# A two-layer encoder: sums of weight quarters for the down projection made ahead, in DRAM

## The chip, the cores and the metric

The kernel runs on one core of a Trainium2 chip. The metric is device time in microseconds of one execution; times shown are medians over runs. The engines are named as in the profile: PE (TensorE matmul), PEld (its weight loads), DVE (VectorE), ACT (ScalarE), POOL (GpSimd), SP (SyncE, which here only issues DMAs).

## The reference

A batch of one sequence of 512 tokens with 1024 features passes two layers. The mixer of layer 0 is neighbourhood attention over an 8 x 64 grid of tokens, that of layer 1 a mixture of three dilated sliding-window attentions. Everything is float32. Cut to what matters here:

```python
D_MODEL, SEQ, DEPTH = 1024, 512, 2
D_FF = 2816

def swiglu(x, w_gate, w_up, w_down):
    return (jax.nn.silu(x @ w_gate) * (x @ w_up)) @ w_down

# every layer:
#   x += post_norm(mixer(pre_norm(x)))
#   x += post_norm(swiglu(pre_norm(x)))
```

The change concerns `@ w_down`, a product of a 512 x 2816 matrix with a 2816 x 1024 one, once in each layer.

## The kernel before, in words

The program is one long sequence: queries, keys and values with the attention of layer 0; its output projection; gate and up of layer 0; down of layer 0; the same for layer 1 with the dilated attention. A scheduler orders the instructions of each engine by priorities and dependences when the program is built, so neighbouring stages overlap on an engine.

Every large product is done with seven half-size products in place of eight (the method of Strassen and Winograd), and every factor is split into a high and a low part (`split`: an ACT copy, L89, and a DVE subtraction, L90), which `mm3` multiplies in three matmuls, L101 to L103. The products of four quarters need sums of quarters of both factors.

For attention projections and gate and up this is done per unit by the class `Seven`: a unit loads two weight halves of 512 KB (`load2`, L85, on SP's queue), and its method `sums` adds quarters of the weights, two of the additions on POOL (L168, L169, and for some units L170 and L174). Gate and up has 22 units f in each layer, the neighbourhood attention 8 units j of queries and keys, the dilated attention 24 units n.

For the down projection, `down`, the weight `wd` lies in DRAM as four quarters `ga`, `gb`, `ua`, `ub` of 128 x 5632 floats (2·QF, with QF = 2816). The seven products are, in this order: p2 with gb; p1 with ga; d1 with ga+ua; s2 with ga+ua+ub, and between its pieces s4 with ub; s3 with ua+ub; x2b with all four. The chain's names of tiles carry them: `h_d0p`, `l_d0p` are the high and low parts for p1 and p2 of layer 0, `h_d0d` those for d1, `h_d0s` for s2, s3 and s4, `h_d0x2b` for x2b; layer 1 has `h_d1...`. Each product goes in 6 pieces, five of 128 x 1024 floats (512 KB, 12 matmuls of 128 x 512) and one of half that. The results gather in the PSUM tiles `yd_s` (left) and `yd_pp` (right).

Before, the sums are made within the down projection. The arena `mem` (named `wd`) holds ga, which SP loads with L652; accumulating DMAs of POOL's queue (L604, in `add`) put ua onto it for d1, ub for s2, gb for x2b. For s3 a piece of ua is loaded into a ring buffer and ub accumulated onto it. That is 24 accumulating DMAs a layer. Plain loads (L610, in `loaded`) go through a ring of four half buffers `r_d`, the same memory that gate and up's units use, and from d1 on two more in the arena `more` (named `raw`).

The arenas `wd` and `raw` reuse the memory of `fg`, which gate and up used; the last instruction that reads `fg` is L568, the product that makes the last tile of `hid`, the input of down.

Of the kernel before, what the change touches and what calls it, by code (L numbers as in the profile page):

```python
# [12 lines left out]
F32 = mybir.dt.float32  # L13
# [25 lines left out]
def encoder_kernel(ctx: ExitStack, tc: tile.TileContext, a: dict, out: bass.AP):  # L39
# [88 lines left out]
    class Seven:  # L128
# [36 lines left out]
        def sums(self):  # L165
            q, e = self.q, self.adds
            self.w22 = split(*self.v, q[3])
            e[0].tensor_add(q[0], q[0], q[2])  # L168
            e[1].tensor_add(q[2], q[2], q[3])  # L169
            e[2].tensor_add(q[3], q[0], q[3])  # L170
            self.w12 = self.pair("b", self.q3[:, 0:4:3])
# [367 lines left out]
        pre(3)  # L539
        ops(3)  # L540

    def gate_up(layer, xs, hid, fg):
        wg, wu = a["wg"], a["wu"]
        raws = ring(fg, 0, 2 * D, 3)
        g_, u_, p5_ = ring(fg, 6 * D, 512, 4), ring(fg, 8 * D, 512, 2), ring(fg, 9 * D, 256, 2)
        v_ = w22_ring(rxc[:, 4 * D:5 * D])
        units, us = {}, {}

        def unit_of(f):
            if f in units or f >= FT:  # L550
                return units.get(f)
            raw = load2((wg[layer, f], wu[layer, f]), f"gu{layer}_{f}", None if f % 5 < 2 else next(raws))
            b, g = bank(("s", "s", "pp", "o", "pp", "pp")[f % 6], f"gu{layer}_{f}"), next(g_)

            def sink(n, left, other):
                u = us.get(f)
                if n == 0:
                    act.activation(g[:, :256], other, AF.Copy)
                    dve.tensor_add(g[:, :256], g[:, :256], left)
                elif n == 1:  # L560
                    act.activation(u[:, :256], other, AF.Copy)
                    dve.tensor_sub(u[:, :256], u[:, :256], left)  # L562
                elif n == 2:
                    dve.tensor_sub(u[:, 256:], other, left)
                else:
                    act.activation(g[:, :256], g[:, :256], AF.Silu)
                    act.activation(g[:, 256:], left, AF.Silu)
                    dve.tensor_mul(hid[f], *(v.rearrange("p (h c) -> p h c", h=2) for v in (g, u)))  # L568

            units[f] = Seven(raw, b, xs, f"{layer}_{f}", sink, None, next(v_), (pool, pool, dve, dve))  # L570
            return units[f]

        ahead = 3
        for f in range(ahead):
            unit_of(f).first()
        for f in range(FT):
            for i in range(f, min(f + 2, FT)):
                if i not in us:
                    us[i], units[i].p5 = next(u_), next(p5_)
            run(unit_of(f), unit_of(f + 1), unit_of(f + ahead))  # L580

    def down(layer, hm, hl_, mem, yp, more, sink):
        left, right = ([bank(u, f"yd{layer}_{u}{m}") for m in range(2)] for u in ("s", "pp"))
        x1a, x1b, x2a, x2b = (hm[:, i * QF:(i + 1) * QF] for i in range(4))
        pieces = [slice(2 * i, min(2 * i + 2, FT // 2)) for i in range(FT // 4 + 1)]
        last = len(pieces) - 1  # L590
        raws = [wpool.tile([P, 2 * D], F32, tag="raw", name=f"r_d{layer}{i}", bufs=2) for i in range(2)]
        raws = [r[:, i * D:i * D + D] for i in range(2) for r in raws]
        raw_ = cycle(raws)
        ga, gb, ua, ub = (a["wd"][layer, i] for i in range(4))

        def xp(v, i):
            return v[:, pieces[i].start * 256:pieces[i].stop * 256]

        def wp(v, i):
            return v[:, pieces[i].start * 512:pieces[i].stop * 512]  # L600

        def add(v, src):

            nc.gpsimd.dma_start(v, src, accum_op=ALU.add)  # L604

        def loaded(w, more=None):
            for i in range(w.shape[1] // D + (w.shape[1] % D > 0)):
                c = slice(i * D, min((i + 1) * D, w.shape[1]))
                v = next(raw_)[:, :c.stop - c.start]
                nc.sync.dma_start(v, w[:, c])  # L610
                if more is not None:
                    add(v, more[:, c])
                yield v

        def added(w):

            for i in range(last + 1):
                add(wp(mem, i), wp(w, i))
                yield wp(mem, i)

        def operands2(x, w, name):
            h, u = next(hl_), wslot(name)
# [23 lines left out]
            prod(right, operands2(xp(x1b, i), w, f"{nm}p2_{i}"), i == 0)  # L646
        for m in range(2):
            act.activation(y1g[m], right[m], AF.Copy)

        early = list(loaded(ga[:, :2 * D]))  # L650
        for i in (*range(2, last + 1), 0, 1):
            nc.sync.dma_start(wp(mem, i), wp(ga, i))  # L652
        for i in range(last + 1):
            w = early[i] if i < len(early) else wp(mem, i)
            prod(left, operands2(xp(x1a, i), w, f"{nm}p1_{i}"), i == 0)
            dve.tensor_sub(xp(x2a, i), xp(x2a, i), xp(x2b, i))
        for m in range(2):
            dve.tensor_add(y1g[m], y1g[m], left[m])
        raw_ = cycle(raws + [more[:, i * D:i * D + D] for i in range(2)])
        for i in range(last + 1):  # L660
            t = wp(mem, i)
            add(t, wp(ua, i))
            prod(right, operands2(xp(x2a, i), t, f"{nm}d1_{i}"), i == 0)
            dve.tensor_sub(xp(x2a, i), xp(x2a, i), xp(x1a, i))
        for m in range(2):
            act.activation(p5[m], right[m], AF.Copy)
        ops = None
        for i, w in enumerate(loaded(ub)):
            w0 = wp(ub, i)
            t = wp(mem, i)  # L670
            add(t, w0)
            dve.tensor_add(xp(x1b, i), xp(x2a, i), xp(x1b, i))

            dve.scalar_tensor_tensor(xp(x1a, i), xp(x2a, i), -1.0, xp(x2b, i), op0=ALU.mult, op1=ALU.subtract)
            prod(left, operands2(xp(x2a, i), t, f"{nm}s2_{i}"))
            if ops:
                prod(right, ops)
            ops = operands2(xp(x1b, i), w, f"{nm}s4_{i}")
        for m in range(2):
            act.activation(y1u[m], left[m], AF.Copy)  # L680
        prod(right, ops)
# [24 lines left out]
        for n in range(2):  # L706

            kept = []
            for i, w in enumerate(loaded(ua, ub) if n == 0 else added(gb)):
                ops = operands2(xp((x1a, x2b)[n], i), w, f"{nm}{('s3', 'x2b')[n]}_{i}")  # L710
                if i > last - 2:
                    kept.append(ops)
                else:
                    prod(left, ops)
                for f, *t in steps.get((n, i), ()):
                    f(*t)
            if n == 0:
                for m in range(2):
                    for ops in kept:
                        prod(left, ops, False, (m,))  # L720
                    act.activation(y2u[m], left[m], AF.Copy)
                for m in range(2):
                    dve.tensor_sub(y2u[m], p5[m], y2u[m])
# [47 lines left out]
    def ffn(layer, stack):  # L771
        hl_ = ring(rxc, 0, D, 5)
        rxb = None
        with arena(f"hid{layer}", FT * 512, "right") as hm:
            h2 = hm.rearrange("p (h x) -> p h x", h=2)
            hid = [h2[:, :, f * 256:f * 256 + 256] for f in range(FT)]
            with arena(f"fg{layer}", 9 * D + 512) as fg:
                gate_up(layer, xs, hid, fg)
            with arena(f"ed{layer}", D, "right") as ed, arena(f"yp{layer}", 2 * D, "right") as yp:
                rcomb = ring(ed, 0, 512, 2)  # L780

                def sink(t, xt, hs, gn):
                    if layer == 1:
                        for n in range(2 if t == NT - 1 else 1):
                            s = slice(512 * n, 512 * n + 512) if t == NT - 1 else ALL
                            (nc.sync, act)[n].dma_start(out[t][:, s], xt[:, s])
                    else:
                        nc.sync.dma_start(spill[1][t], xt)
                        prenorm(hs[t], xt, gn, f"n{layer}_{t}")
                        operands(mixer_operands(rxb) if rxb is not None else None, x, hs, t, rcomb, f"n{layer}_{t}")  # L790

                with arena(f"wd{layer}", 2 * QF) as mem, arena(f"raw{layer}", 2 * D) as more:
                    end = down(layer, hm, hl_, mem, yp, more, sink)
                if layer == 0:
                    rxb = stack.enter_context(arena("rxb1", 6 * D, dtype=F32R))
                end()
        return rxb


    stack = ExitStack()  # L800
# [39 lines left out]

    for j in range(PAIRS):
        run(unit_of(j), unit_of(j + 1), unit_of(j + 1))
        q = next(q_).rearrange("p (h t) -> p h t", h=2)
        split_q(q[:, :, 64:], qs[j])
        pool.tensor_copy(q[:, :, 0:64], q[:, :, SEQ:].bitcast(F32))
# [248 lines left out]
    for n, i in enumerate(order):  # L1094
# [4 lines left out]
        nxt = unit_of(order[n + 1]) if n + 1 < len(order) else None  # L1099
        cs, js = between()  # L1100
        run(unit_of(i), nxt, nxt, cs)
        if g == 0:
            q = q_.rearrange("p (h t) -> p h t", h=2)
            split_q(q, qs)
            if j == 0:
                zero_rows(kl_)
            kd, kl = split_k(k_, kl_, ks)
# [108 lines left out]
```

## Time and profile before

| what | value |
|---|---|
| median of 3 runs | 1610.05 us (1607.22 to 1615.42) |
| the profiled execution | 1605.1 us |
| its span in the trace | 1603.3 us |
| PE / DVE / ACT / POOL busy | 93% / 75% / 56% / 39% |
| DMA, mean | 209 MB, 130 GB/s |

The profile is of one execution; times in its rows are microseconds from the start of the span, durations are microseconds unless marked ns. A row of the chain has start, length, engine, tile, line; a row of a tile has minimum, median and maximum ns and the first and last start. SPq and POOLq are the issuing sides of those engines' DMA queues.

### The profile page before, as it was taken

Reading aid. Unit: us, or ns where it says so; the run is one execution under the profiler, and the core shown is the slowest. Engines: PE = TensorE matmul, PEld = TensorE weight load, DVE = VectorE, ACT = ScalarE, POOL = GpSimd, SP = SyncE. Lnnn points to the kernel's source line nnn. Section 1 sums busy time; section 2 is a strip of 40 time slices with the busy share of each in tenths; the row PEclk is TensorE's granted clock in tenths of the full one; section 3 lists DMA queues with packets and bytes.
Section 4 is the critical chain, followed back from the end, with each engine's and each line's share of the span. In section 5 each row is a group of like instructions: output and inputs, shape, how many; then the busy total and the mean of one; then the engine's idle time right before and its main releaser. Section 6 shows DMA issues by size and latency. Waiting matters only on the chain.

```text
span 1603.3 us, 28068 instructions
## 1 busy us (share of the span) xinstructions
PE 1486.7 (93%) x10788; PEld 1366.7 (85%) x10788; DVE 1205.0 (75%) x1884; ACT 897.6 (56%) x1787; POOL 628.1 (39%) x500
## 2 busy tenths in 40 slices
PE   7999898899999898889999999999887899999896
PEld 7988776899999786879999988988766899999774
DVE  5488966799998867677677776776536699998866
ACT  5367753555555556434467776676654555555554
POOL 3356434533330222566555443544104533330221
PEclk9999999999999999999999999999998999999999
DMA  4323455133323995534322322322626133323993
GB/s 171 109 80 105 150 191 197 66 106 106 106 80 99 256 243 172 173 132 159 109 95 62 121 81 92 133 67 61 222 88 197 66 106 106 106 80 102 265 244 112
DMA packets 77766, 208.99 MB, mean 130 GB/s; under 512 B 18560, under 2 KB 28800, under 8 KB 77632
## 3 DMA queue, kind: packets, MB, share of 16 engines
q1 hardware_dynamic: 65456, 165.11, 30.5%
q0 software_dynamic: 12032, 41.82, 10.9%
q8 instruction: 85, 1.39, 0.4%
q14 instruction: 49, 0.40, 0.1%
q10 hardware_dynamic: 144, 0.26, 0.0%
HBM read 185.04 MB, written 22.12 MB: 129 GB/s over the span
## 4 chain that ended last, share of the span: by engine, by line
PE 61%; DVE 12%; DMA 11%; issue 6%; ACT 5%; POOL 4%; SPq 1%; POOLq 0%; DVEq 0%; ACTq 0%
PE gu L101 9%; PE gu L102 9%; PE gu L103 9%; PE pp_d L101 4%; PE pp_d L102 3%; PE pp_d L103 3%; DMA raw<-wd 3%; DMA wd<-wd 2%; PE t L1046 2%; PE sb L986 1%; ACT ap L1032 1%; PE vd L102 1%; PE vd L101 1%; PE vd L103 1%; PE yd_pp L101 1%
## 5 line engine op out<-in xcount | busy, mean ns | idle before, releaser
L103 PE MATMUL gu<-rxc,l_a 128*128 128x256 f32 x352 | 102.0, 290 | 3.3 <-DVE l_a L90 3.3
L102 PE MATMUL gu<-rxc,h_a 128*128 128x256 f32 x352 | 102.4, 291 | 0.0
L101 PE MATMUL gu<-rxc,h_a 128*128 128x256 f32 x352 | 102.1, 292 | 0.1
L101 PE MATMUL gu<-rxa,h_c 128*128 128x256 f32 x352 | 100.2, 285 | 0.7 <-DVE fg L562 0.4
L101 PE MATMUL gu<-rxa,h_b 128*128 128x256 f32 x352 | 99.7, 284 | 0.7 <-ACT rxa L324 0.7
L102 PE MATMUL gu<-rxa,h_b 128*128 128x256 f32 x352 | 99.8, 284 | 0.0
L103 PE MATMUL gu<-rxa,l_c 128*128 128x256 f32 x352 | 99.6, 283 | 0.0
L102 PE MATMUL gu<-rxa,h_c 128*128 128x256 f32 x352 | 99.6, 283 | 0.0
L103 PE MATMUL gu<-rxa,l_b 128*128 128x256 f32 x352 | 99.5, 283 | 0.0
L604 POOL DMA_DIRECT2D wd<-wd x36 | 34.3, 995 | 137.8 <-DVE l_d0p L90 49.7
L168 POOL TENSOR_TENSOR fg<-fg 128x512 f32<-128x512 f32 x24 | 39.8, 1659 | 120.9 <-DVE l_a L90 119.7
L954 ACT ACTIVATE ap<-ap 128x256 f32<-128x256 f32 x128 | 63.9, 502 | 31.4 <-DVE ap L953 30.8
L168 POOL TENSOR_TENSOR r_d<-r_d 128x512 f32<-128x512 f32 x24 | 39.7, 1656 | 105.9 <-DVE l_ad L90 97.7
L168 POOL TENSOR_TENSOR r_gu<-r_gu 128x512 f32<-128x512 f32 x20 | 35.5, 1773 | 115.8 <-DVE l_a L90 115.8
L89 ACT ACTIVATE rxc<-hid 128x512 fp32r<-128x512 f32 (+1 forms) x84 | 49.2, 591 | 54.1 <-PE yd_s L102 33.6
L103 PEld LDWEIGHTS gu<-rxc,l_a 128*128 128x128 f32 x352 | 70.0, 199 | 3.7 <-DVE l_a L90 3.7
L101 PEld LDWEIGHTS gu<-rxc,h_a 128*128 128x128 f32 x352 | 69.8, 199 | 0.6 <-ACT rxc L324 0.6
L102 PEld LDWEIGHTS gu<-rxc,h_a 128*128 128x128 f32 x352 | 70.0, 199 | 0.0
L101 PEld LDWEIGHTS gu<-rxa,h_c 128*128 128x128 f32 x352 | 67.5, 192 | 1.7 <-DVE fg L562 1.5
L101 PEld LDWEIGHTS gu<-rxa,h_b 128*128 128x128 f32 x352 | 67.6, 193 | 1.0 <-ACT rxa L324 1.0
L102 PEld LDWEIGHTS gu<-rxa,h_c 128*128 128x128 f32 x352 | 67.5, 192 | 0.2
L103 PEld LDWEIGHTS gu<-rxa,l_b 128*128 128x128 f32 x352 | 67.6, 192 | 0.0
(599 smaller groups left out, 6265.2 us busy)
## 6 DMA issues: line engine op xcount, KB each, us to landing
r_d<-dil_qk SPq DMA_DIRECT2D x48, 512.0 KB, 4.5
r_d<-wd SPq DMA_DIRECT2D x30, 512.0 KB, 4.4
wd<-wd POOLq DMA_DIRECT2D x30, 512.0 KB, 10.4
fg<-wg SPq DMA_DIRECT2D x24, 512.0 KB, 3.7
fg<-wu SPq DMA_DIRECT2D x24, 512.0 KB, 4.6
r_gu<-wg SPq DMA_DIRECT2D x20, 512.0 KB, 3.7
r_gu<-wu SPq DMA_DIRECT2D x20, 512.0 KB, 4.6
r_n<-na_qk SPq DMA_DIRECT2D x16, 512.0 KB, 4.5
```

The source lines that it names most:

```text
L89: act.activation(h, src, AF.Copy)
L101: i = pe.matmul(o, s[0], m[0], start=start, stop=False, skip_group_check=True)
L102: pe.matmul(o, s[0], m[1], start=False, stop=False, skip_group_check=True)
L103: pe.matmul(o, s[1], m[0], start=False, stop=stop, skip_group_check=True)
L168: e[0].tensor_add(q[0], q[0], q[2])
L604: nc.gpsimd.dma_start(v, src, accum_op=ALU.add)
L954: act.activation(pr[:, f], pr[:, f], AF.Exp, bias=st[:, c:c + 1], scale=-1.0, accum_out=st[:, c + 2:c + 3])
L986: pe.matmul(ss[hd][:, f0:f0 + P], qf[rw, block(c)], kf[rw, block(c)], start=True, stop=True)
L1032: act.activation(v, v, AF.Copy, scale=w[:, 2 * b + hd:2 * b + hd + 1])
L1046: pe.transpose(t[:, block(i)], part(a_b, *blocks[4 * n + i]), ident)
```

## The change

The sums are made in two DRAM tensors, `wsum0` and `wsum1`, one for each layer, each with four slots of 128 x 5632 floats: gu = ga+ua, gub = gu+ub, uab = ua+ub, and every = gub+gb. `wd_sums` gives 16 steps for a layer, each one DMA on POOL's queue over half a slot (128 x 2816 floats): 8 copies and 8 accumulating DMAs. Each step is ordered behind the first POOL addition (L168) of some unit, by `after`, which sets the order of two instructions on the same engine without a semaphore. Layer 0: one step in each of the first 6 attention units, and one in every second unit of gate and up, 10 in all. Layer 1: one step in each dilated unit from n = 4 on, 16 in all; gate and up of layer 1 has none. `down` then only loads (L626), 42 pieces a layer; the arena `wd` is gone, `more` has six buffers instead of two, and one ring of ten buffers serves all seven products.

```diff
         def sums(self):
             q, e = self.q, self.adds
             self.w22 = split(*self.v, q[3])
-            e[0].tensor_add(q[0], q[0], q[2])
+            self.added = e[0].tensor_add(q[0], q[0], q[2])
...
             run(unit_of(f), unit_of(f + 1), unit_of(f + ahead))
+            if sums and f % 2 == 0:
+                sums.pop(0)(units[f].added)
...
+    wsum = [dpool.tile([4, P, 2 * QF], F32, name=f"wsum{i}") for i in range(2)]
+
+    def wd_sums(layer):
+        ga, gb, ua, ub = (a["wd"][layer, i] for i in range(4))
+        gu, gub, uab, every = (wsum[layer][i] for i in range(4))
+
+        def step(o, v, h, add, anchor):
+
+            c = slice(h * QF, h * QF + QF)
+            more = dict(accum_op=ALU.add, max_dma_last_dim=2 * QF) if add else {}
+            after(nc.gpsimd.dma_start(o[:, c], v[:, c], **more), anchor)
+
+        return [partial(step, o, v, h, add) for pairs, add in ((((gu, ga), (uab, ua)), False),
+                (((gu, ua), (uab, ub)), True), (((gub, gu),), False), (((gub, ub),), True),
+                (((every, gub),), False), (((every, gb),), True)) for h in range(2) for o, v in pairs]
...
-        raw_ = cycle(raws)
+        raw_ = cycle(raws + [more[:, i * D:i * D + D] for i in range(6)])
...
-                if more is not None:
-                    add(v, more[:, c])
+        def loaded(w):
+            for i in range(last + 1):
+                v = next(raw_)[:, :wp(w, i).shape[1]]
+                nc.sync.dma_start(v, wp(w, i))
                 yield v
...
-        early = list(loaded(ga[:, :2 * D]))
-        for i in (*range(2, last + 1), 0, 1):
-            nc.sync.dma_start(wp(mem, i), wp(ga, i))
-        for i in range(last + 1):
-            w = early[i] if i < len(early) else wp(mem, i)
+        for i, w in enumerate(loaded(ga)):
             prod(left, operands2(xp(x1a, i), w, f"{nm}p1_{i}"), i == 0)
...
-        for i in range(last + 1):
-            t = wp(mem, i)
-            add(t, wp(ua, i))
-            prod(right, operands2(xp(x2a, i), t, f"{nm}d1_{i}"), i == 0)
+        for i, w in enumerate(loaded(gu)):
+            prod(right, operands2(xp(x2a, i), w, f"{nm}d1_{i}"), i == 0)
...
-        for i, w in enumerate(loaded(ub)):
-            w0 = wp(ub, i)
-            t = wp(mem, i)
-            add(t, w0)
+        for i, (w, w0) in enumerate(zip(loaded(gub), loaded(ub))):
...
-            for i, w in enumerate(loaded(ua, ub) if n == 0 else added(gb)):
+            for i, w in enumerate(loaded(uab if n == 0 else every)):
...
     for j in range(PAIRS):
         run(unit_of(j), unit_of(j + 1), unit_of(j + 1))
+        if j < 6:
+            sums[0].pop(0)(us[j].added)
...
         run(unit_of(i), nxt, nxt, cs)
+        if n >= 4 and sums[1]:
+            sums[1].pop(0)(us[i].added)
```

The built programs show how the instructions moved. First SP at the start of down in layer 0. A row has the line, the operation, the tile written and the source; `r_d00` and `r_d01` are the two early buffers, whose halves are the ring's first four; `raw0` is the arena `more`; rows that read alike are counted. Before:

```order
L610 DMA r_d00_5452<-wd 128x1024 x2
L610 DMA r_d01_5453<-wd 128x1024 x2
L610 DMA r_d00_5452<-wd 128x1024
L610 DMA r_d01_5453<-wd 128x512
L610 DMA r_d00_5452<-wd 128x1024
```

Those are gb's six pieces and the first of ga; the loads into the arena `wd0` (L652) follow four loads later. After the change:

```order
L626 DMA r_d00_5466<-wd 128x1024 x2
L626 DMA r_d01_5467<-wd 128x1024 x2
L626 DMA r_d00_5466<-wd 128x1024
L626 DMA r_d01_5467<-wd 128x512
L626 DMA r_d00_5466<-wsum0_81 128x1024
L626 DMA r_d01_5467<-wsum0_81 128x1024
L626 DMA raw0_5461<-wd 128x1024
L626 DMA raw0_5461<-wd 128x512
L626 DMA raw0_5461<-wd 128x1024 x4
```

The first two rows are still gb's pieces 0 to 3, but the next two are now pieces 4 and 5 of ga, then pieces 0 and 1 of gu; pieces 4 and 5 of gb and 0 to 3 of ga are loaded last, into `raw0`.

PE at the end of p2's piece 4 in layer 0, from its last row; names with `p2` and `p1` are the products, the digit behind them the piece. Before:

```order
L103 MATMUL yd0_pp1_5451<-h_d0p2_4_5531,rxc_77 128x512
L101 MATMUL yd0_s0_5448<-h_d0p1_0_5572,rxc_77 128x512
L101 MATMUL yd0_s1_5449<-h_d0p1_0_5572,rxc_77 128x512
L102 MATMUL yd0_s0_5448<-l_d0p1_0_5573,rxc_77 128x512
L103 MATMUL yd0_s0_5448<-h_d0p1_0_5572,rxc_77 128x512
```

After:

```order
L103 MATMUL yd0_pp1_5465<-h_d0p2_4_5545,rxc_77 128x512
L101 MATMUL yd0_pp0_5464<-h_d0p2_5_5564,rxc_77 128x512
L101 MATMUL yd0_pp1_5465<-h_d0p2_5_5564,rxc_77 128x512
L102 MATMUL yd0_pp0_5464<-l_d0p2_5_5565,rxc_77 128x512
L103 MATMUL yd0_pp0_5464<-h_d0p2_5_5564,rxc_77 128x512
L102 MATMUL yd0_pp1_5465<-l_d0p2_5_5565,rxc_77 128x512
L103 MATMUL yd0_pp1_5465<-h_d0p2_5_5564,rxc_77 128x512
L101 MATMUL yd0_s0_5462<-h_d0p1_0_5579,rxc_77 128x512
```

Piece 4 of p2 is followed by piece 5 and then by p1, where p1 began right behind piece 4 before.

POOL at the start of gate and up in layer 0 (`r_gu0_0` and `fg0` are weights of its first units, L308 and L346 to L352 belong to norms and the output projection before it). Before:

```order
L169 TENSOR_TENSOR r_gu0_0_2891<-r_gu0_0_2891 128x512
L168 TENSOR_TENSOR r_gu0_1_2926<-r_gu0_1_2926 128x512
L308 TENSOR_TENSOR rs_o0_2_2730<-v_o0_2_2728,mhalf_71 128x1
L169 TENSOR_TENSOR r_gu0_1_2926<-r_gu0_1_2926 128x512
L346 TENSOR_TENSOR ep0_2456<-ep0_2456 128x512
```

After:

```order
L168 TENSOR_TENSOR r_gu0_0_2899<-r_gu0_0_2899 128x512
L596 DMA wsum0_81<-wd 128x2x1408
L169 TENSOR_TENSOR r_gu0_0_2899<-r_gu0_0_2899 128x512
L168 TENSOR_TENSOR r_gu0_1_2934<-r_gu0_1_2934 128x512
L308 TENSOR_TENSOR rs_o0_2_2738<-v_o0_2_2736,mhalf_71 128x1
L169 TENSOR_TENSOR r_gu0_1_2934<-r_gu0_1_2934 128x512
L308 TENSOR_TENSOR rs_yo0_3_2839<-v_yo0_3_2837,mhalf_71 128x1
L346 TENSOR_TENSOR ep0_2464<-ep0_2464 128x512
```

The accumulating DMA (L596) now stands between the unit's two additions, so L169 of that unit is issued behind it.

More of the change, by code (lines that the diff above doesn't have):

```diff
@@ L540, in out_proj, with gate_up @@
         ops(3)
-    def gate_up(layer, xs, hid, fg):
+    def gate_up(layer, xs, hid, fg, sums):
         wg, wu = a["wg"], a["wu"]
@@ L580, in gate_up, with down @@
             run(unit_of(f), unit_of(f + 1), unit_of(f + ahead))
-    def down(layer, hm, hl_, mem, yp, more, sink):
+            if sums and f % 2 == 0:
[11 more added lines that the diff above has]
+                (((every, gub),), False), (((every, gb),), True)) for h in range(2) for o, v in pairs]
+    def down(layer, hm, hl_, yp, more, sink):
         left, right = ([bank(u, f"yd{layer}_{u}{m}") for m in range(2)] for u in ("s", "pp"))
@@ L592, in down @@
         raws = [r[:, i * D:i * D + D] for i in range(2) for r in raws]
-        raw_ = cycle(raws)
+        raw_ = cycle(raws + [more[:, i * D:i * D + D] for i in range(6)])
         ga, gb, ua, ub = (a["wd"][layer, i] for i in range(4))
+        gu, gub, uab, every = (wsum[layer][i] for i in range(4))
         def xp(v, i):
@@ L600, in wp @@
             return v[:, pieces[i].start * 512:pieces[i].stop * 512]
[L602 to L610, printed above, removed]
-                if more is not None:
-                    add(v, more[:, c])
+        def loaded(w):
+            for i in range(last + 1):
+                v = next(raw_)[:, :wp(w, i).shape[1]]
+                nc.sync.dma_start(v, wp(w, i))
                 yield v
-        def added(w):
-            for i in range(last + 1):
-                add(wp(mem, i), wp(w, i))
-                yield wp(mem, i)
         def operands2(x, w, name):
@@ L658, in down @@
             dve.tensor_add(y1g[m], y1g[m], left[m])
-        raw_ = cycle(raws + [more[:, i * D:i * D + D] for i in range(2)])
-        for i in range(last + 1):
-            t = wp(mem, i)
-            add(t, wp(ua, i))
-            prod(right, operands2(xp(x2a, i), t, f"{nm}d1_{i}"), i == 0)
+        for i, w in enumerate(loaded(gu)):
+            prod(right, operands2(xp(x2a, i), w, f"{nm}d1_{i}"), i == 0)
             dve.tensor_sub(xp(x2a, i), xp(x2a, i), xp(x1a, i))
@@ L667, in down @@
         ops = None
-        for i, w in enumerate(loaded(ub)):
-            w0 = wp(ub, i)
-            t = wp(mem, i)
-            add(t, w0)
+        for i, (w, w0) in enumerate(zip(loaded(gub), loaded(ub))):
             dve.tensor_add(xp(x1b, i), xp(x2a, i), xp(x1b, i))
             dve.scalar_tensor_tensor(xp(x1a, i), xp(x2a, i), -1.0, xp(x2b, i), op0=ALU.mult, op1=ALU.subtract)
-            prod(left, operands2(xp(x2a, i), t, f"{nm}s2_{i}"))
+            prod(left, operands2(xp(x2a, i), w, f"{nm}s2_{i}"))
             if ops:
                 prod(right, ops)
-            ops = operands2(xp(x1b, i), w, f"{nm}s4_{i}")
+            ops = operands2(xp(x1b, i), w0, f"{nm}s4_{i}")
         for m in range(2):
@@ L777, in ffn @@
             with arena(f"fg{layer}", 9 * D + 512) as fg:
-                gate_up(layer, xs, hid, fg)
+                gate_up(layer, xs, hid, fg, sums[layer])
             with arena(f"ed{layer}", D, "right") as ed, arena(f"yp{layer}", 2 * D, "right") as yp:
@@ L790, in sink @@
                         operands(mixer_operands(rxb) if rxb is not None else None, x, hs, t, rcomb, f"n{layer}_{t}")
-                with arena(f"wd{layer}", 2 * QF) as mem, arena(f"raw{layer}", 2 * D) as more:
-                    end = down(layer, hm, hl_, mem, yp, more, sink)
+                with arena(f"raw{layer}", 6 * D) as more:
+                    end = down(layer, hm, hl_, yp, more, sink)
                 if layer == 0:
@@ L797, in ffn @@
         return rxb
+    sums = [wd_sums(layer) for layer in range(2)]
     stack = ExitStack()
```

## The prediction

> **What bounds the kernel now.** I read the page first, then the span cut by stage, then the chain, the waits and the tiles of the two down projections.
>
> ```profile
> PE 1486.7 (93%) x10788; PEld 1366.7 (85%) x10788; DVE 1205.0 (75%) x1884; ACT 897.6 (56%) x1787; POOL 628.1 (39%) x500
> PE 61%; DVE 12%; DMA 11%; issue 6%; ACT 5%; POOL 4%; SPq 1%; POOLq 0%; DVEq 0%; ACTq 0%
> ```
> ```profile
> 300.00:503.00 203.00, 200.97 (x1665) 200.12 (x1665) 183.26 (x225) 106.64 (x183) 65.86 (x37) 1.00 0.27 89
> 503.00:645.00 142.00, 128.58 (x611) 105.71 (x609) 104.39 (x140) 78.94 (x123) 29.53 (x31) 0.96 0.81 218
> 770.00:1200.00 430.00, 407.36 (x3259) 373.21 (x3257) 295.61 (x636) 286.36 (x717) 180.92 (x142) 0.98 0.31 102
> 1465.00:1603.00 138.00, 118.77 (x541) 95.91 (x540) 95.56 (x129) 69.68 (x109) 26.60 (x29) 0.97 0.78 202
> ```
>
> The first fence is busy time and the chain by engine, the second the span in stretches: length, busy us of PE, PEld, DVE, ACT and POOL, clock, DMA share, GB/s. TensorE bounds the whole. Gate and up of layer 0 (300 to 503) leaves it 2 us idle and the DMA engines 73%; the dilated attention (770 to 1200) leaves PE 23 us. The two down projections (503 to 645, 1465 to 1603) are the other way round: DMA is 0.81 and 0.78 busy, and PE idles 13 and 19 us. That is all this change can win there; what it loses it loses in the stretches with free DMA.
>
> What waits in the down projections, by the waits (total, times, longest), the tiles (ns; first and last start) and the chain of layer 0:
>
> ```profile
> PE yd_pp L101 <- ACT h_d0d L89: 5.2, 1, 5.2
> PE yd_pp L101 <- ACT h_d1d L89: 4.7, 1, 4.7
> ```
> ```profile
> L101 PE MATMUL yd_pp<-h_d0d,rxc x22: 387/389/797, 549.5 to 566.0; 128*128 128x512 f32 x22
> L101 PE MATMUL yd_pp<-h_d1d,rxc x22: 389/389/697, 1509.2 to 1525.5; 128*128 128x512 f32 x22
> L103 PE MATMUL yd_s<-h_d0s,rxc x44: 388/389/628, 567.4 to 619.7; 128*128 128x512 f32 x44
> L103 PE MATMUL yd_s<-h_d1s,rxc x44: 388/389/397, 1526.8 to 1575.9; 128*128 128x512 f32 x44
> ```
> ```profile
> 536.32 12.00 DMA wd<-wd
> ...
> 602.73 11.97 DMA raw<-wd
> ```
> ```profile
> 525.01 0.39 PE L101 MATMUL yd_pp<-h_d0p,rxc 128*128 128x512 f32 x1
> 527.73 0.61 PE L101 MATMUL yd_s<-h_d0p,rxc 128*128 128x512 f32 x2
> ```
>
> The first `yd_pp` of the last fence is the first of 12 matmuls of piece 4 of p2, the `yd_s` the first of p1: 12 matmuls in 2.72 us, 0.227 us each, so a product of 66 is 15.0 us. d1 waited 5.2 us for a sum (the 12.00 us accumulate on the chain), then took 549.5 to 566.7 (three more matmuls after the last L101), 17.2 us: 2.2 over the 15.0. Layer 1: 4.7, and 16.9 us, 1.9 over. The rows of `yd_s<-h_d0s` span s2, s4 and s3: 194 matmuls between first and last, 44.1 us of work in 52.3 us, 8.1 us lost; layer 1, in 49.1 us, 5.0 lost. s3 is where the ring's loads are followed by an accumulate (the 11.97 us step). So the sums cost TensorE 7.4 + 8.1 us in layer 0 and 6.6 + 5.0 in layer 1.
>
> The clock stands beside it, in slices of 10 us:
>
> ```profile
> 610.00:620.00 10.00, 8.17 (x27) 5.67 (x25) 6.58 (x10) 6.29 (x10) 1.44 (x2) 0.83 0.83 305
> 620.00:630.00 10.00, 8.46 (x42) 7.13 (x42) 9.33 (x12) 8.90 (x18) 3.46 (x2) 1.00 0.22 77
> ```
>
> Clock 0.83 while s3 starves, 1.00 when it is fed. I read the 2.2 and 1.9 us of d1 as matmuls restarting at a lower clock after the stall. [...]
>
> **The change, part by part.** *(1) A new stall at piece 4 of p2.* Before, pieces 4 and 5 of gb went to the early buffers `r_d`. Now they are the first loads into `more`, whose memory was gate and up's `fg`; the load waits for the last L568, which reads `fg`. Before, that wait sat ahead of L652's loads for p1, with two early p1 pieces in hand.
>
> ```profile
> 524.57 1.23 DVE L90 TENSOR_TENSOR l_d0p<-r_d,h_d0p 128x1024 fp32r<-128x1024 f32 x1 [1.81 <-ACT h_d0p L89]
> 525.71 0.68 DVE L568 TENSOR_TENSOR hid<-fg 128x512 f32<-128x512 f32 x1
> ```
> ```profile
> 526.42 2.96 SPq L652 DMA_DIRECT2D wd<-wd  x6
> ```
> ```profile
> 531.35 1.06 ACT L89 ACTIVATE h_d0p<-wd 128x1024 fp32r<-128x1024 f32 x1 [1.13 <-DMA wd<-wd]
> ```
>
> Issue to the ACT split is 526.42 to 531.35, 4.9 us, the split 1.06. In the new order L568 no longer stands behind that l_d0p: it can run at 524.57 and end at 525.25, so the load lands at 530.2, the split ends at 531.3, and PE, ready at 525.0, waits 6.3 us. With layer 0's restart of 2.2 that is 8.5 against 7.4 in d1: **+1.1**. Layer 1, where the order is the same, 6.3 + 1.9 against 6.6: **+1.6**. d1 then has its sums ready and its own stall goes.
>
> *(2) s3 on plain loads.* −8.1 and −5.0. What is late next is DVE: in the slice after s3 it is 9.33 of 10 busy, so I give back 1 us in each layer (0 to 3): **−7.1, −4.0**. Removing 24 issues a layer from POOL wins nothing more: POOL is 29.53 busy of 142 there. The longer ring's loads replace others one for one, and their issue on SP overlaps matmuls.
>
> *(3) The sums' traffic.* A step moves 128x2816 floats, 1.44 MB. Prices, accumulates alone and plain loads alone:
>
> ```profile
> q0 software_dynamic: 1354, 4.43, 104.7%
> ```
> ```profile
> q1 hardware_dynamic: 4896, 17.83, 26.2%
> ```
>
> The first is 548 to 570: 4.43 MB in 22 us, 0.20 MB/us, so 7.2 us a step. The second is 300 to 503: 17.83 MB in 26.2% of 203 us, 0.335 MB/us, so 4.3 us. The trace has no transfer from DRAM to DRAM; below, a step could cost the plain 4.3 us, above, the 12.00 us that 512 KB took on the chain, 34 us for 1.44 MB. I take the streams, since a step's queue is full by itself: 8 x 7.2 + 8 x 4.3 = 92 us of the 16 engines a layer. Even at 34 us the next step on the same sum is 2 to 4 units later, so no step blocks POOL, and all sums of a layer stand before down needs them.
>
> *(4) POOL's issues.* A step is issued between a unit's L168 and L169. Existing prices:
>
> ```profile
> L604 POOL DMA_DIRECT2D wd<-wd x36: 838/865/1552, 534.0 to 1551.5; - x36
> ```
> ```profile
> L765 POOL DMA_DIRECT2D rxa<-rvd x14: 527/578/715, 166.1 to 1179.0; - x14
> ```
>
> A copy is 0.58 us; an accumulate, cut into 256 rows of 1408 where L604 has 128, 0.87 to twice that, 1.73. In the middle of the attention the chain does not go through POOL; at its start it does, and at the start of gate and up too:
>
> ```profile
> 66.97 1.30 POOL r_n L168
> ```
> ```profile
> 265.08 2.28 POOL r_gu L168
> ...
> 267.44 2.15 POOL r_gu L169
> ```
>
> One copy on the first: **+0.6** (0 to 3.5, all six exposed). Two accumulates on the second (the units of f = 0 and 2), 1.7 to 3.5: **+2.5**. Later units of gate and up are covered by POOL's idle (65.86 of 203 busy); without it, eight more issues of about 0.9 us, +7.
>
> *(5) The dilated attention, 16 units.*
>
> ```profile
> L168 POOL TENSOR_TENSOR r_d<-r_d x24: 1262/1292/2357, 765.3 to 1115.1; 128x512 f32<-128x512 f32 x24
> ```
> ```profile
> 1007.23 6.38 DMA r_d<-dil_qk
> ...
> 1036.72 1.67 DMA ap<-sw
> ```
> ```profile
> sw<-ap SPq DMA_DIRECT2D x8, 8.0 KB, 1.4
> sw<-ap SPq DMA_DIRECT2D x8, 4.0 KB, 1.4
> ```
>
> 24 units in 350 us are 15.2 us each; units 4 to 19 run from about 826 to 1065, 240 us, of which steps fill 92: 38%. The swaps through `sw` cost 1.4 us at 4 KB and at 8 KB alike: latency, which I leave. The weight load of 6.38 us on the chain doubles with a chance of 38%: **+2.4** (0 if hidden; 14 or more below).
>
> *(6)* The loads of `r_d` for the next layer behind down come later in SP's order; the chain of before does not hang on them: 0 (to +2).
>
> Sum: 1.1 + 1.6 − 7.1 − 4.0 + 0.6 + 2.5 + 2.4 = −2.9 us. The profiled execution took 1605.1 us (its span is 1603.3); it would take 1602.2. The median of the runs, 1610.05, is 4.95 above, so **1607**.
>
> **Rivals.** *B, the new steps are wholly hidden and DVE gives nothing back:* −2.9 − 5.5 − 2.0 = −10.4, **1600**. For it: DMA share 0.27 in gate and up, POOL 39% busy. Against: POOL stands on the chain at both starts.
>
> *C, slower: transfers of the dilated attention are slowed by the steps.* Weight loads there have little slack:
>
> ```profile
> 915.96 0.80 SPq L85 DMA_DIRECT2D r_d<-dil_qk  x2
> ```
> ```profile
> 920.07 1.04 ACT L89 ACTIVATE h_ad<-r_d 128x1024 fp32r<-128x1024 f32 x1
> ```
>
> ACT splits a load 4.1 us after the issue, about as soon as it has landed. 16 units x 2 loads x 4.1 us x 38% is 50 us of lengthening; if 40% is exposed, +20 in place of 2.4: **1625**. It decides (over 1618) from 13 us, some quarter exposed. Against: the chain of before has one such load in this stretch. [...]
>
> *D, the stall of (1) does not come* (fg is free earlier than L568 as I read it): both layers gain 8.5 and 8.2 more, **1590**. Against: the wait of L652 behind L568 in the rows above.
>
> **How the numbers follow.** A, my sum, 0.46; B 0.23; C 0.20; D 0.06; 0.05 for what I do not see, either way. A itself is 1601 to 1615, from the small terms' bounds. The range, 1593 to 1625, leaves out D, half of C's far side and the unseen. A measurement tells about 0.5%, 8 us: faster means under 1602, slower over 1618. Faster: most of B, D, a little of A: 0.32. Slower: most of C and the tail of A: 0.23. Same: 0.45.
>
> **What would show it.** Right: no wait of `yd_pp` on h_d0d, one of about 6 us on h_d0p; s3 close to 15 us; L596 steps of 4 to 8 us, issues of 0.6 and 0.9 to 1.7 us; the down stretches some 6 and 2 us shorter, gate and up's start 2 to 3 longer. Wrong: steps of DRAM to DRAM far longer than 7 us, new waits of ACT on `r_d` between 826 and 1065, or POOL waiting on its own DMA.

## The result, and the profile after

The changed kernel took 1629.67 us (median of 4 runs, 1622.79 to 1639.76) against 1608.86 for the kernel before (4 runs, 1607.22 to 1615.42): ratio 1.0129, 95% interval 1.0106 to 1.0153. It is slower by 21 us, where 1607 was forecast with a range up to 1625.

First the page of the changed kernel: busy time and the chain by engine, then its new transfers (KB each, median us from issue to landing; the first of these two rows mixes 8 plain copies with the 16 accumulates, the second is copies alone).

```profile
PE 1502.6 (92%) x10788; PEld 1381.6 (85%) x10788; DVE 1218.4 (75%) x1884; ACT 903.2 (55%) x1787; POOL 602.7 (37%) x484
PE 53%; DVE 10%; DMA 6%; ACT 5%; issue 5%; POOL 4%; SPq 1%; POOLq 0%; DVEq 0%; ACTq 0%
wsum<-wd POOLq DMA_DIRECT2D x24, 1408.0 KB, 11.9
wsum<-wsum POOLq DMA_DIRECT2D x8, 1408.0 KB, 7.5
```

The same stretches as before, in the same columns (length, busy us of PE, PEld, DVE, ACT, POOL, clock, DMA share, GB/s). Everything now comes later, by 18 us at the first down projection and 32 at the second, so the stretches no longer cut exactly at the stages; the DMA share is what to read.

```profile
300.00:503.00 203.00, 197.82 (x1625) 196.25 (x1624) 183.65 (x218) 105.92 (x179) 86.20 (x55) 0.99 0.54 160
503.00:645.00 142.00, 136.90 (x708) 116.99 (x707) 114.06 (x159) 84.56 (x135) 9.36 (x6) 0.98 0.54 177
770.00:1200.00 430.00, 398.91 (x3187) 367.26 (x3186) 305.38 (x603) 277.38 (x676) 186.54 (x156) 0.98 0.53 157
1465.00:1603.00 138.00, 133.39 (x736) 116.35 (x736) 111.24 (x153) 79.80 (x125) 9.69 (x6) 0.98 0.50 162
```

The traffic moved as meant: down fell from 0.81 and 0.78 to 0.54 and 0.50, gate and up rose from 0.27 to 0.54, the dilated attention from 0.31 to 0.53. In down the change does what it says. The waits of PE in the two layers, the tiles of d1, s2 and s3, and one slice of 10 us:

```profile
PE yd_pp L101 <- ACT h_d0p L89: 4.4, 1, 4.4
```
```profile
PE yd_pp L101 <- ACT h_d1p L89: 4.5, 1, 4.5
```
```profile
L101 PE MATMUL yd_pp<-h_d0d,rxc x22: 389/389/389, 569.2 to 583.0; 128*128 128x512 f32 x22
L103 PE MATMUL yd_s<-h_d0s,rxc x44: 389/389/392, 584.8 to 628.8; 128*128 128x512 f32 x44
L103 PE MATMUL yd_s<-h_d1s,rxc x44: 388/389/389, 1560.2 to 1604.2; 128*128 128x512 f32 x44
```
```profile
540.00:550.00 10.00, 5.56 (x25) 4.02 (x24) 4.79 (x8) 4.23 (x7) 0.00 (x0) 0.78 0.63 226
```

The wait on h_d0d is gone and one on h_d0p, at piece 4 of p2, has come; the slice holds it, with the clock at 0.78. s2, s4 and s3 now take 44.0 us in both layers where they took 52.3 and 49.1. From the first p2 matmul to the last of x2b, layer 0 went from 128.2 to 118.3 us and layer 1 from 125.2 to 118.8: 16 us gained. The spans of the two profiled executions, 1603.3 and 1630.2 us, differ by 27 us the other way, so 43 us were lost where down is not: by the starts of the tiles, 15 us up to the first units of gate and up of layer 0, and 24 us more between the first dilated unit and the end of the projection behind it.

### The profile page after: what moved, and what is told of

It reads as the page before. It is cut to its first block, busy times and chain, and to the rows that moved or that the text cites. A ratio compares the mean times of both kernels' runs of the same rounds, so it can differ in the third digit from the quotient of the medians.

```text
span 1630.2 us, 28061 instructions
## 1 busy us (share of the span) xinstructions
PE 1502.6 (92%) x10788; PEld 1381.6 (85%) x10788; DVE 1218.4 (75%) x1884; ACT 903.2 (55%) x1787; POOL 602.7 (37%) x484
## 4 chain that ended last, share of the span: by engine, by line
PE 53%; DVE 10%; DMA 6%; ACT 5%; issue 5%; POOL 4%; SPq 1%; POOLq 0%; DVEq 0%; ACTq 0%
PE gu L101 8%; PE gu L102 8%; PE gu L103 8%; PE pp_d L101 3%; PE pp_d L103 3%; PE pp_d L102 3%; PE t L1047 2%; PE yd_pp L101 2%; PE yd_pp L102 2%; PE yd_pp L103 2%; PE yd_s L101 1%; PE yd_s L102 1%; PE yd_s L103 1%; DMA sw<-ap 1%; PE o L1055 1%
## 5 line engine op out<-in xcount | busy, mean ns | idle before, releaser
L168 POOL TENSOR_TENSOR r_d<-r_d 128x512 f32<-128x512 f32 x24 | 39.6, 1650 | 122.0 <-DVE l_ad L90 116.5
L168 POOL TENSOR_TENSOR fg<-fg 128x512 f32<-128x512 f32 x24 | 39.9, 1662 | 120.6 <-DVE l_a L90 119.3
L168 POOL TENSOR_TENSOR r_gu<-r_gu 128x512 f32<-128x512 f32 x20 | 36.0, 1798 | 114.5 <-DVE l_a L90 114.5
L90 DVE TENSOR_TENSOR rxc<-hid,rxc 128x512 fp32r<-128x512 f32 (+1 forms) x84 | 53.8, 642 | 19.3 <-ACT rxc L89 19.0
```

Of the source, the lines that this page charges most:

```text
L90: dve.tensor_sub(l, src, h.bitcast(F32))
L168: self.added = e[0].tensor_add(q[0], q[0], q[2])
```

## The experiments

The program is put in order by a scheduler that simulates a timeline (`schedule_with_timeline_sim=True` where the kernel is built), transfers included. Steps added to its timeline give the attentions another order of matmuls, which the prediction did not price. So there were two theories. ORDER says that the new order of instructions costs the time, TRAFFIC that the steps' transfers do. To part them, four kernels were run together; the kernel before took 1609.94 beside them.

**no_sums**: the gain alone. It makes no sums, and down loads quarters of the weight in their place.

```diff
-        gu, gub, uab, every = (wsum[layer][i] for i in range(4))
+        gu, gub, uab, every = ga, gb, ua, ub
...
-        if j < 6:
-            sums[0].pop(0)(us[j].added)
```

(and the other two places that issue steps likewise.)

> The changed kernel without the 32 steps; down loads the quarters of wd themselves where it loaded sums (ga for gu, gb for gub, ua for uab, ub for every), so the loads are the same in number and size and no sum is made. In attention and in gate and up no engine gets an instruction less or more than in the kernel before. Between the marks of the two traces the changed kernel gained about 10 us in down of layer 0 and 6 in layer 1 and lost some 43 elsewhere. Theory ORDER (the loss is the scheduler's: it plans with modelled transfer times, and the steps in its plan gave attention another order) and theory TRAFFIC (the loss is the steps' transfers in the DMA engines and queues) both expect here the gain alone: 1609 - 16 = about 1593, within 4.

1587.5, ratio 0.9859 (0.9838 to 0.9879). The medians differ by 22 us, the spans of the two profiled executions by 17 (1603.3 and 1586.4), and by the tiles those lie in down, 9.8 and 7.5.

**order_of_before**: all steps, the order of no_sums. At the end of the program each engine's instructions are chained by edges that set order and add no wait, in the order read from the built no_sums; a step stands behind its anchor. In its trace every engine's instructions, the steps aside, follow one another by operation and tile as in no_sums.

```diff
-            after(nc.gpsimd.dma_start(o[:, c], v[:, c], **more), anchor)
+            STEPS.append((nc.gpsimd.dma_start(o[:, c], v[:, c], **more), anchor))
...
         encoder_kernel(tc, aps, out)
+        pin(tc, nc)
...
+    for k in order:
+        i = ins[k]
+        for v in (i, behind.get(i.name)):
...
+            if e in last:
+                tc.add_manual_dep(v, last[e], NoSync, reason="pinned")
+            last[e] = v.name
```

> The changed kernel with all its 32 steps and sums, but every engine's other instructions held, by ordering edges that make no engine wait for another, in the order of the kernel without steps; each step stands right behind its anchor on POOL. ORDER: the loss goes with the order, what stays is POOL's issues and a little contention, 1593 + 3 to 8 = 1596 to 1601, faster than before. TRAFFIC: the loss stays, 1622 to 1632.

1626.02, ratio 1.0100 (1.0080 to 1.0119): 38 us over no_sums, in the same order of instructions. That is TRAFFIC's number. The chaining by itself was not run on no_sums; held_small_steps below is chained in the same way and lies 8 us over no_sums, so it adds no more than that.

**order_of_after_no_sums**: no steps, chained in the order of the changed kernel.

> The kernel without steps (no sums, down loads the quarters themselves), every engine's instructions held in the order of the changed kernel. ORDER: the loss comes without any step, 1618 to 1630. TRAFFIC: the order is harmless and the time that of the kernel without steps, 1593 within 5.

1611.27, ratio 1.0017 (0.9999 to 1.0034): 24 us over no_sums without any step. So ORDER is true as well, between its bound and the rival's: each theory alone was too simple. The two do not add up: 24 for the order, then 18 for the steps in that order; or 38 for the steps, then 4 for the order. The steps cost less in the scheduler's new order, but with them in place the new order is not faster than the old one (1629.67 and 1626.02, with intervals that overlap).

Where it lies, from first and last starts of the tiles of one profiled execution each, in us over no_sums (the last two columns are the experiments that follow). A stage ends at the first matmul of gate and up's product `gu<-rxa,h_b`, at the first of p2, at the first of `pp_d` (the first dilated unit's product), at the last of `yo` (the projection) and at the last of x2b:

| stage | order of before, steps | order of after, no steps | changed kernel | held, small steps | held, copies |
|---|---|---|---|---|---|
| attention 0 and its projection | +7.7 | +6.2 | +13.1 | +1.6 | +6.1 |
| gate and up 0 | +1.3 | +3.8 | +3.2 | +1.1 | −0.1 |
| down 0 to the first dilated unit | +1.5 | +0.5 | +1.9 | +2.6 | +1.5 |
| dilated units and projection 1 | +28.9 | +9.7 | +25.7 | −0.7 | +12.0 |
| the rest | −1.8 | −0.2 | −1.7 | −1.1 | −1.9 |
| sum | +37.6 | +20.0 | +42.2 | +3.5 | +17.6 |

**gate_up_only**: all steps where loads have slack.

```diff
-            if sums and f % 2 == 0:
+            if sums and f < 16:
                 sums.pop(0)(units[f].added)
...
-        if j < 6:
-            sums[0].pop(0)(us[j].added)
...
-        if n >= 4 and sums[1]:
-            sums[1].pop(0)(us[i].added)
```

> The changed kernel with all 16 steps of a layer in gate and up of that layer, one in each unit f = 0 to 15, none in attention. The order of the attentions is then that of the kernel before. ORDER: attention loses nothing, the start of gate and up pays POOL's issues and a reshuffled tail of the projection, 1593 + 4 to 8 in two layers = 1597 to 1609. TRAFFIC: gate and up's loads have 8 us of slack and the steps fill about 92 of 200 us, so the loss is small too, 1595 to 1603. It tells the two apart little; it says whether the place matters.

1596.76, ratio 0.9911 (0.9888 to 0.9934): the same sums (32 steps) cost 9 us here instead of 42. Landing of loads from 310 to 450, first in no_sums, then here:

```profile
fg<-wg SPq DMA_DIRECT2D x9, 512.0 KB, 3.7
fg<-wu SPq DMA_DIRECT2D x9, 512.0 KB, 4.5
```
```profile
fg<-wg SPq DMA_DIRECT2D x9, 512.0 KB, 9.3
fg<-wu SPq DMA_DIRECT2D x9, 512.0 KB, 10.8
```

The weight loads take 6 us longer and TensorE does not notice: the first matmul of down in layer 0 starts at 509.3, and at 510.0 in no_sums. It is not the length of the transfers that costs here, but the slack at the place. The 7.7 us between the two spans (1586.4 and 1594.1) lie elsewhere: some 3 from there to the first dilated unit, some 3 up to the end of the projection of layer 1, some 3 behind it. What makes them is open.

Next: what in the traffic costs, and the stall at p2. The kernel before took 1608.88 beside these.

**held_small_steps** and **held_copies** split order_of_before:

```diff
-            STEPS.append((nc.gpsimd.dma_start(o[:, c], v[:, c], **more), anchor))
+            o2, v2 = (t[:, c].rearrange("p (n x) -> p n x", n=2 if add else 1)[:, :, :QF // 44] for t in (o, v))
+            STEPS.append((nc.gpsimd.dma_start(o2, v2, **more), anchor))
```
```diff
-            STEPS.append((nc.gpsimd.dma_start(o[:, c], v[:, c], **more), anchor))
+            STEPS.append((nc.gpsimd.dma_start(o[:, c], v[:, c]), anchor))
```

> All engines' order held as in the kernel without steps, all 32 steps issued at their anchors, but each over 64 columns of every row it had (1/22 of the bytes, as many rows), and down loads the quarters themselves. It parts POOL's issues from the bytes. BYTES (packets of the steps hold up swaps and weight loads): the loss of 38 us goes with the bytes, 1588 + 1 to 5 = about 1591. ISSUE (about 1 us of POOL between two additions, 16 times a layer, and what waits for POOL): most of the loss stays, 1615 to 1626.

> All engines' order held as in the kernel without steps; each accumulating step is a plain copy of the same bytes in its place (no sum is made). It halves the rows of an issue and takes the accumulate's extra time out of the DMA engines: by the prices of the prediction 16 x 4.3 = 69 us of engine time a layer in place of 92. BYTES in proportion: 1588 + 38 x 0.75 = about 1616. If it is the accumulates that hold engines, clearly less, 1595 to 1608. ISSUE: issues halve, about 1607.

Small steps: 1595.96, ratio 0.9923 (0.9898 to 0.9947), 8 us over no_sums. Copies: 1612.06, ratio 1.0017 (1.0002 to 1.0031), 25 us over. So POOL's issues and their rows, with the chaining, are worth some 8 us of the 38, the bytes some 30. With copies in place of the 16 accumulates 25 of the 38 us stay, near the 1616 expected of bytes in proportion. Less than half of the dilated loss stays (12.0 of 28.9), and all but 1.6 of the loss in attention 0, whose six steps are four copies and two accumulates.

What the steps hold up in the dilated attention: exchanges through `sw` from 830 to 1230 (KB each, median us to landing), and pieces of the chain there (start, length); each pair first in no_sums, then with the steps in the same order:

```profile
sw<-ap SPq DMA_DIRECT2D x8, 4.0 KB, 1.4
sw<-ap SPq DMA_DIRECT2D x7, 8.0 KB, 1.4
```
```profile
sw<-ap SPq DMA_DIRECT2D x8, 4.0 KB, 2.9
sw<-ap SPq DMA_DIRECT2D x7, 8.0 KB, 2.4
```
```profile
976.13 1.39 DMA sw<-ap
978.87 1.62 DMA ap<-sw
```
```profile
1010.60 8.53 DMA sw<-ap
1020.81 5.09 DMA ap<-sw
```

Transfers of a few KB, most of which had taken 1.4 to 1.8 us (the longest 5.6), take up to 8.5, and they lie on the chain in pairs. It hits some and not most: the median of the reads back (`ap<-sw`) stays at 1.7 and 1.8. ACT's waits for them (total, times, longest), again without and with steps:

```profile
ACT ap L1029 <- DMA ap<-sw: 2.3, 2, 1.3
```
```profile
ACT ap L1035 <- DMA ap<-sw: 19.8, 4, 9.9
```

With copies these waits are 10.1 us, with small steps 1.0. One exchange of order_of_before shows what moved while it waited. It is issued at 1072.60, when SP's last two weight loads, issued before 1066.6, have landed (median 4.0 us), while a step issued at 1065.99 needs 12.7 us, until 1078.7. From 1072.6 to 1076.0 the only queue that moves anything is POOL's (packets, MB, share of 16 engines), and the exchange lands at 1078.9:

```profile
wsum<-wd POOLq DMA_DIRECT2D x1, 1408.0 KB, 12.7
q0 software_dynamic: 123, 0.69, 103.1%
```
```profile
1072.60 6.31 DMA sw<-ap
```

So for 3.4 of its 6.31 us nothing moved but the step on the other queue, and no load of its own queue was under way; it landed 0.2 us after the step. The one of 8.53 us, too, was issued as the loads before it landed, with a step under way. A lower clock goes with the loss: its mean over the span was 0.977 in no_sums and is 0.967 here. An estimate from these two is that it makes at most 1% of the 1625.7 us, 16 us; how much of that fell on matmuls is not parted from the waits themselves.

In the first attention it is a weight load, from 60 to 215 in no_sums and with the steps, and on the chain:

```profile
r_n<-na_qk SPq DMA_DIRECT2D x12, 512.0 KB, 4.2
```
```profile
r_n<-na_qk SPq DMA_DIRECT2D x12, 512.0 KB, 6.0
```
```profile
70.26 7.33 DMA r_n<-na_qk
```

**no_swaps_no_sums** and **no_swaps_held_steps** ask whether the small transfers are the whole of it; the kernel before took 1610.73 beside them. They leave out the exchange between partitions: a DVE copy within the partition stands in its place.

```diff
-        nc.sync.dma_start(d[:, :4 * n], in_)
-        for k in range(4):
-            nc.sync.dma_start(out_[32 * k:32 * k + 32].rearrange("p (i s) -> p i s", s=n),
-                              d[:, n * k:n * k + n].rearrange("(i p) s -> p i s", i=4))
+        dve.tensor_copy(out_, in_)
```

> The kernel without steps and sums, and without the exchange of softmax statistics across partitions through sw (each exchange, five small DMAs one after another, is a DVE copy within the partition). It is the base of the next run. Both theories: the swaps on its chain, some 1.4 + 1.7 us each with SP's issues, go: 1588 - 5 to 25.

> The same without the exchange, but with all 32 steps and sums, every engine's other instructions held in the order of that base. With the exchange, steps in a held order cost 38 us, 29 of them between the first dilated unit and the end of the projection. SWAPS (the small transfers wait in the DMA engines behind the steps' packets, and a chain of two of them decides a unit): the 29 fall under 10, and the whole difference to the base is 10 to 18. LOADS (512 KB weight and value loads come late): the 29 stay at 20 or more, the difference 30 or more.

1591.26, ratio 0.9888 (0.9871 to 0.9904), and 1617.99, ratio 1.0047 (1.0026 to 1.0068). The base did not get faster without its swaps, against both theories (the scheduler ordered it otherwise, so it is a base for its own pair alone). The steps cost 27 us instead of 38, and in the dilated units 13.6 instead of 28.9: under LOADS' 20 and over SWAPS' 10. So the swaps are about half, as far as two bases with different orders can be compared; the 17.5 us that ACT waits longer for them above are of the same size. What is left stands beside slower weight loads, from 830 to 1100, without and with steps, and a wait of ACT with steps (total, times, longest; lines of the held kernels stand two lower):

```profile
r_d<-dil_qk SPq DMA_DIRECT2D x34, 512.0 KB, 4.4
```
```profile
r_d<-dil_qk SPq DMA_DIRECT2D x34, 512.0 KB, 6.5
```
```profile
ACT h_ad L91 <- DMA r_d<-dil_qk: 8.7, 5, 3.3
```

With the swaps in place the same loads went from a median of 4.5 to 5.0 us and from a longest of 6.2 to 12.0. That the loads make the whole of the other half is argued, not shown.

**gate_up_early_ring** takes the stall out of p2: gate_up_only, with the first eight pieces in the four early buffers.

```diff
-        raw_ = cycle(raws + [more[:, i * D:i * D + D] for i in range(6)])
+        raw_ = chain(raws * 2, cycle([more[:, i * D:i * D + D] for i in range(6)] + raws))
```

> The kernel with the steps in gate and up (1596.8), and in down the six pieces of gb and the first two of ga go through the four early buffers, as before the change; the six buffers in the memory of gate and up's fg come after them. If the stall at piece 4 of p2 is what the prediction made it, 8.5 us in each layer with the restart, it goes: 1597 - 14 to 17 = 1580 to 1583. Rival: the loads behind it are late instead, p1 waits for its third piece and nothing is gained, 1594 to 1599.

1580.99, ratio 0.9833 (0.9806 to 0.9860), and 15.8 us under gate_up_only: by the tiles 7.4 of them in down of layer 0 and 7.0 in layer 1. PE's waits in down of layer 0 no longer hold one on h_d0p. It is faster than the kernel before and the changed kernel. That it is 6.5 us under no_sums says little of the steps, since no_sums still has the stall at p2.

**gate_up_early_ring_held** chains the same kernel in the order of its twin without steps.

> The same kernel, every engine's other instructions held in the order that the scheduler gives without steps. The steps in gate and up cost 9 us over the kernel without sums. ORDER of the places around gate and up: 3 to 6 us less than the kernel it is compared with, about 1577. If it is the steps' transfers there: no difference, or some us more, since the order is then not fitted to them.

1585.48, ratio 0.9856 (0.9837 to 0.9874): 4.5 us over the unheld kernel, with intervals that overlap. It is the second of the two outcomes, since holding the order gains nothing. That the scheduler's answer to the steps is a gain here is not shown.

**gate_up_4_to_19** moves the steps away from gate and up's start.

```diff
-            if sums and f < 16:
+            if sums and f >= 4:
```

> The early ring with the steps in units 4 to 19 of gate and up instead of 0 to 15, away from the start where POOL's additions are on the chain (two issues of about 1.15 us per two units there). If those issues are what is left, 1581 - 2 to 5 = about 1577; if the left cost is a reshuffled order, no difference; the last steps now end two units before down, and a wait of d1 or x2b for a sum would show as a loss, 1585 or more.

1581.71, ratio 0.9824 (0.9801 to 0.9847): no difference from gate_up_early_ring. But two things changed: the trace has every engine's instructions in the order of gate_up_early_ring_held, which has its steps in units 0 to 15 and took 3.8 us more, with intervals that just overlap. A cost of 2.5 us of POOL's issues at the start, which the prediction gave, is neither shown nor excluded.

## Why the prediction was wrong, point by point

- *(1) the new stall at p2.* Right in place, near in size. From the first matmul of p2 to that of p1 layer 0 went from 19.4 to 27.9 us, 8.5 more, of which 1.4 are the six matmuls of piece 5 that now come first: 7.1 for the stall with its restart, and 7.7 in layer 1, against the 8.5 and 8.2 forecast. The wait itself was 4.4 us in place of 6.3: the load was split 3.7 us after its issue, where I had taken 4.9 from L652, and L568 ended just before PE ran dry, not just after. The restart, what the stall has over the wait, was longer in turn: 2.7 us, and 3.2 in layer 1 (7.7 less a wait of 4.5), where I had 2.2 and 1.9. It is the lower clock: after the wait the granted clock was 0.50 from 546 to 552 us in layer 0 and from 1522 to 1528 in layer 1, and the matmuls of 128x512 there started 0.43 us apart, and 0.23 once the clock was back at 1.00. Before, behind d1's wait of 5.2 us in layer 0, it was 0.50 from 549 to 553. The early ring won 14.4 us in the two layers' down, where rival D had 16.7.
- *(2) s3 on plain loads.* Right in kind, too small: −8.3 and −5.1 for the rows of s2 to s3, −1.1 and −2.2 from there to the end of x2b, where I gave 1 us back to DVE in each. Down gained 9.9 and 6.4, forecast 6.0 and 2.4.
- *(3) and (4), prices.* An accumulate's issue took 1.15 us, a copy's 0.58 (forecast 0.87 to 1.73, and 0.58):

```profile
L596 POOL DMA_DIRECT2D wsum<-wd x24: 537/1153/1239, 57.7 to 1075.3; - x24
L596 POOL DMA_DIRECT2D wsum<-wsum x8: 555/578/625, 321.2 to 1042.2; - x8
```

  The accumulates landed in 12.2 us and the copies in 7.3 (medians of 16 each in the changed kernel), where I had 7.2 and 4.3 of pure streaming, beside other traffic, and POOL was not blocked by them (no engine waited for L596, and the eight semaphore instructions of POOL's queue there took 17 ns each). (My upper bound from the chain, 34 us, is 33 by its own numbers.) But I took issue as the only cost in attention 0: +0.6 forecast, +13.1 measured, 7.7 with the steps in the old order and 6.2 with the new order alone.
- *(5) the dilated attention, the step that failed.* "The swaps through `sw` cost 1.4 us at 4 KB and at 8 KB alike: latency, which I leave." That the time was 1.4 us at both sizes says that bytes did not limit it there; it does not say that it is immune to a queue: with the steps in the held order the medians were 2.9 and 2.4 us. Priced at nothing, the swaps turned out about half of the 28.9 us that the steps cost there in the held order; what is left, with the loads in it, was priced at 2.4 (the changed kernel lost 25.7 there). Rival C had the right side and the right kind at 1625, with a chance of 0.20 that was too low, and named the loads alone. That a load beside a step takes twice its time, which is behind the 2.4 and behind rival C's 50 us, is shown by no run: it was an assumption of mine. In its place the runs showed 512 KB loads of the dilated attention, from 830 to 1100, at a median of 4.4 us and at most 6.4 before, 6.0 and at most 12.5 in the changed kernel; those of gate and up at 3.7 and, with all steps there, 9.3; a swap that took 8.5 us where the median without steps is 1.4; and one that saw nothing of its queue move for 3.4 us while the step's did.
- *What was not in the sum at all:* the order. The fences on the order showed only down and gate and up's start, and I costed the rest as if the instructions had stayed. PE's order differs from that of no_sums through both attentions. The order alone is 24 us, which leaves 1611.27, inside the range; the traffic in the old order is 38 and gives 1626.02, past it. So it is the price of the traffic that failed the range, and the new order came on top without adding much to it.

That I called 1607 came of counting gains where the trace shows waits, and counting losses only on today's chain: a chain tells who is late now, not who has no slack.

## What to carry to other kernels

Before moving traffic into a stage with free DMA, ask for the slack of each transfer there, the small ones first: the same sums cost 42 us with 22 of their 32 steps in attention, where the exchanges, and some of the loads, are used as they land, and 9 us with all in gate and up, where loads took 6 us longer and the matmuls behind them came no later. Where a scheduler plans with modelled transfers, an added DMA can move instructions far from it: hold the order to find out which of the two costs you. And when a ring is lengthened with memory that another stage frees late, give its first pieces to buffers that are free early.

## What was not expected of the hardware

A transfer of 4 to 8 KB grew from 1.4 us to as much as 8.5 us beside 1.4 MB steps on another queue, while the median of 512 KB loads beside them only went from 4.4 us before to 6.0 in the changed kernel (from 830 to 1100). In gate and up of layer 0, 512 KB loads went from 3.7 to 9.3 us, more than doubled, and the matmuls of down behind them came no later. Accumulates from DRAM to DRAM landed in 12.2 us for 1408 KB; those of 512 KB onto SBUF, several of them under way together, took 10.4 before: from issue to landing 8.7 ns a KB against 20.3.
